# Up projections of a conv-gated FFN: high weights against high and low activations in one matmul of 512 columns

## The chip, the cores and the metric

The kernel runs on one core of one Trainium2 chip. The metric is the device time of one execution in microseconds (us). Before the change it is 771.88 us, the median of three runs (771.77 to 773.24).

## What is computed

The program is a decoder trunk of two layers over 256 tokens and a model width of 1024: a Mamba-2 mixer and an FFN, then shared keys and values, a dilated attention and a second FFN, and a last RMSNorm. The change is in the up projections of the two FFNs. All inputs and outputs are float32.

```
D_MODEL, SEQ, FFN_DIM, FFN_CONV = 1024, 256, 2816, 3

def _conv_ffn(h, w_up, conv_w, w_down):
    u = _causal_depthwise_conv(h @ w_up, conv_w)
    gate, val = u[..., :FFN_DIM], u[..., FFN_DIM:]
    return (jax.nn.silu(gate) * val) @ w_down

x = x + _conv_ffn(_rms_norm(x, ffn_norm[layer]), ffn_w_up[layer], ffn_conv_w[layer], ffn_w_down[layer])
```

## The kernel before

Every large product is done in three matmuls of a reduced-precision float32 type (F32R in the code). A weight tile is split into a high part `wh` (a cast on ScalarE, L98) and a low part `wl` (the weight minus its high part, on DVE, L100). The activations are split in the same way into `xnh` and `xnl`. The product is high times high, plus high weights times low activations, plus low weights times high activations; the low times low part is left out. L273, L274 and L275 (in `mm3`) are these three, each with 128 rows of contraction, 128 output channels and 256 columns, the tokens.

An up projection has 44 tiles of 128 channels. They are taken as 22 pairs, j = 0 to 21: tile j of the gate half and tile j of the value half. One DMA brings the weights of a pair (1 MB). A tile takes eight steps, k = 0 to 7, of three matmuls, so a pair takes 16 steps or 48 matmuls. Both tiles of a pair lie in the two halves of one PSUM bank of the tag `acc`, of which there are three. Pairs 0 to 4 multiply activations that are not yet normalised, and the result is scaled after (`u`, L729). In the place of pair 1 the function `normed` makes `xnh` and `xnl` from the normalised activations, and pairs 5 to 21 use these. That is 17 pairs in each layer.

After its matmuls a pair is worked off by `post` (L725): a first tap of the causal convolution on ScalarE for each tile (L311), two more taps for each tile on DVE (L317), a SiLU of the gate on ScalarE (L732), the product of both on DVE (`gf`, L734), and its split into high and low on ScalarE (L738) and DVE (L739), in the tile `gp`. For pairs 5 to 21 the convolution reads PSUM directly.

The weights run ahead of the matmuls. `W.get` for pair j also starts the DMA and the split of pair j + 1 in program order. There are three buffers for raw weights and six each for `wh` and `wl`, so three pairs. The order of instructions on TensorE is that of the code; on ScalarE and DVE a scheduler fixes it when the program is built, and each of these engines then works through its list strictly in that order. The DMAs of weights are issued on SyncE's queue.

The down projection that follows (`res_proj` in layer 0, `out_proj` in layer 1) reads `gp`, whose high and low parts lie next to each other. In `res_proj` (L665, L667) the high weights meet both parts in one matmul of 512 columns, and the low weights meet the high part in one of 256. In layer 1 `turn` transposes parts of the stream X on TensorE behind the matmuls of pairs 6 to 9, into PSUM banks of the tags t1, t2, t4 and t5.

Of the kernel before, what the change touches and what calls it, by code (L numbers as in the profile page):

```python
# [7 lines left out]
F32 = mybir.dt.float32  # L8
# [45 lines left out]
def trunk(ctx, tc, a, out):  # L54
# [145 lines left out]
    class Stream:  # L200
# [5 lines left out]
        def begin(self):  # L206
            self.h = []
            self.l = []
            for i in range(len(self.ws)):
                self.h.append(act.tile([128, KT, T], F32R, tag=f"xh{i}", name="xh"))  # L210
                self.l.append(act.tile([128, KT, T], F32R, tag=f"xl{i}", name="xl"))
            self.acc = act.tile([128, T], F32, tag="sqacc", name="sqacc")
# [94 lines left out]
    def conv(dst, u, w, b, taps):  # L307

        for i in range(2):
            if b is None:  # L310
                ACT.activation(out=dst[:, i, :], in_=u[:, i, :], func=AF.Copy, scale=w[i][:, taps - 1:taps])  # L311
            else:
                ACT.activation(out=dst[:, i, :], in_=u[:, i, :], func=AF.Identity,  # L313
                               scale=w[i][:, taps - 1:taps], bias=b[i])
        for i in range(2):
            for s in range(1, taps):
                r = DVE.scalar_tensor_tensor(out=dst[:, i, s:], in0=u[:, i, :T - s],  # L317
                                             scalar=w[i][:, taps - 1 - s:taps - s],
                                             in1=dst[:, i, s:], op0=ALU.mult, op1=ALU.add)
        return r  # L320

    def normed(w, rb):

        h = act.tile([128, KT, T], F32R, tag="xh1", name="xnh")
        l = act.tile([128, KT, T], F32R, tag="xl1", name="xnl")
        for k in range(KT):
            t = wk.tile([128, T], F32, tag="sq", name="xnt")
            DVE.scalar_tensor_tensor(out=t, in0=X[:, k, :], scalar=P(w)[:, k:k + 1], in1=rb,
                                     op0=ALU.mult, op1=ALU.mult)
            ACT.copy(out=h[:, k, :], in_=t)  # L330
            DVE.tensor_tensor(out=l[:, k, :], in0=t, in1=h[:, k, :].bitcast(F32), op=ALU.subtract)
        return h, l

# [3 lines left out]
    def operands():  # L337

        h = act.tile([128, KT, T], F32R, tag="xh1", name="xnh")
        l = act.tile([128, KT, T], F32R, tag="xl1", name="xnl")  # L340
        for i in range(2):
# [146 lines left out]
    def conv_post(g, n):  # L488
        st = sts[g]
        u = st["po" + n]  # L490
        cv = wk.tile([128, 2, T], F32, tag="cv" + n, name="cv")
# [221 lines left out]
    def ffn(L, S, nxt):  # L713
# [3 lines left out]
        po = {}  # L717
        cw = P(f"fconv{L}")

        def mm(j, i, **kw):  # L720
            if j not in po:
                po[j] = (acc_bank(), W.get(f"w_up{L}", j))
            tile_a(po[j][0][:, i, :], po[j][1][i], *ops[j >= 5], **kw)

        def post(j):  # L725
            u = po[j][0]
            if j < 5:
                u = wk.tile([128, 2, T], F32, tag="C", name="u")
                DVE.tensor_tensor(out=u, in0=po[j][0], in1=nm.row2, op=ALU.mult)  # L729
            cv = wk.tile([128, 2, T], F32, tag="cvbc", name="cv")  # L730
            conv(cv, u, [cw[:, 3 * t:3 * t + 3] for t in (j, j + FT)], None, 3)
# [10 lines left out]
        for j in range(FT):  # L742
# [11 lines left out]
            if j == 1:  # L754
                ops.append(normed(f"ffn_norm{L}", nm.row))
            if nxt is None and 5 < j < 10:
# [221 lines left out]
    def turn(i):  # L978

        c, f = i % 2, i // 2  # L980
        if i == 0:
            tok["x"] = act.tile([128, 2, D], F32, tag="xh0", name="xt")
            tok["w"] = act.tile([128, 2, D], F32, tag="xl0", name="wf")
            SP.dma_start(out=tok["w"][:, 0, :], in_=a["fnorm"].unsqueeze(0).to_broadcast([128, D]))
        pt = ps.tile([128, 512], F32, tag=f"t{(1, 2, 4, 5)[i]}", name="pxt")
        for n in range(4):
# [191 lines left out]
```

## Time and profile before

| what | value |
|---|---|
| median of three runs | 771.88 us |
| the profiled execution, its own time | 771.69 us |
| its span, first to last instruction | 769.6 us |
| TensorE busy | 758.8 us, 99% of the span |
| DVE busy | 605.4 us, 79% |
| ScalarE busy | 461.3 us, 60% |
| DMA bytes | 135.71 MB, mean 176 GB/s |

The profiled execution takes 2.1 us outside of its span and lies 0.2 us under the median. A matmul's listed duration reaches from its start to its modelled end, and the next one starts long before that end; so TensorE's pace is to be read from starts, and its busy share doesn't say how many matmuls it could take in the same time. Durations of DVE and ScalarE overlap a little too: the next instruction's start comes before the listed end of the one ahead.

### The profile page before, as it was taken

The numbers are of one execution on the slowest core, as the hardware profiler recorded it, in microseconds if no ns is written. First come the engines' busy times: TensorE is split into PE (matmuls) and PEld (weight loads), VectorE is DVE, ScalarE is ACT, GpSimd is POOL, SyncE is SP. The second block draws the span as 40 slices with busy tenths as digits, with TensorE's granted clock in tenths as the row PEclk, the third lists the DMA queues.
The fourth block names the chain that finished last, engine by engine and source line by source line (L and its number), as shares of the span: only waits on it lengthen the run. The fifth ranks groups of instructions, "written<-read, shape, count | busy, mean of one in ns | idle before, by whom it ended". The sixth has DMA issues, their size and how long they took to land.

```text
span 769.6 us, 14590 instructions
## 1 busy us (share of the span) xinstructions
PE 758.8 (99%) x5832; PEld 720.5 (94%) x5832; DVE 605.4 (79%) x1062; ACT 461.3 (60%) x776; POOL 97.7 (13%) x89
## 2 busy tenths in 40 slices
PE   8999999999999999999999999999999999999996
PEld 6899999999989999999888999999999999999885
DVE  6989988887588998887677598777588998888452
ACT  6757777775656566565556446556367676565331
POOL 0003635355100000000000131111100000000000
PEclk9999999999999999999999999999999999999999
DMA  8584753433272475545566654353234575554621
GB/s 324 200 301 158 288 187 111 165 110 121 99 278 106 169 270 183 201 151 172 184 206 230 204 175 157 108 192 121 100 118 158 195 271 172 192 185 143 220 75 55
DMA packets 22916, 135.71 MB, mean 176 GB/s; under 512 B 2561, under 2 KB 3873, under 8 KB 8769
## 3 DMA queue, kind: packets, MB, share of 16 engines
q1 hardware_dynamic: 21072, 129.51, 48.3%
q10 hardware_dynamic: 1776, 5.28, 2.0%
q8 instruction: 46, 0.75, 0.4%
q14 instruction: 22, 0.17, 0.1%
HBM read 133.17 MB, written 1.61 MB: 175 GB/s over the span
## 4 chain that ended last, share of the span: by engine, by line
PE 93%; issue 2%; DVE 2%; ACT 1%; DMA 1%; POOL 1%; SPq 0%; POOLq 0%; DVEq 0%
PE po L273 18%; PE po L275 18%; PE po L274 18%; PE po L665 7%; PE po L673 6%; PE po L667 4%; PE fo L1036 2%; PE fo L1037 2%; PE fo L1038 2%; PE py L568 1%; PE po L293 1%; PE po L294 1%; PE po L295 1%; PE s L903 1%; PE s L896 1%
## 5 line engine op out<-in xcount | busy, mean ns | idle before, releaser
L98 ACT CAST wh<-raw 128x1024 fp32r<-128x1024 f32 (+1 forms) x238 | 245.2, 1042 | 201.4 <-PE po L274 114.6
L100 DVE TENSOR_TENSOR wl<-raw,wh 128x1024 fp32r<-128x1024 f32 (+1 forms) x238 | 293.4, 1237 | 78.8 <-ACT wh L98 77.3
L273 PE MATMUL po<-xnh,wh 128*128 128x256 f32 x800 | 226.5, 283 | 0.0
L275 PE MATMUL po<-xnh,wl 128*128 128x256 f32 x800 | 226.0, 282 | 0.0
L274 PE MATMUL po<-xnl,wh 128*128 128x256 f32 x800 | 225.3, 282 | 0.0
L273 PEld LDWEIGHTS po<-xnh,wh 128*128 128x128 f32 x800 | 150.9, 189 | 0.2 <-issue 0.2
L274 PEld LDWEIGHTS po<-xnl,wh 128*128 128x128 f32 x800 | 151.0, 189 | 0.0
L275 PEld LDWEIGHTS po<-xnh,wl 128*128 128x128 f32 x800 | 150.1, 188 | 0.0
L273 PE MATMUL po<-xh,wh 128*128 128x256 f32 x400 | 115.3, 288 | 0.0
L275 PE MATMUL po<-xh,wl 128*128 128x256 f32 x400 | 113.1, 283 | 0.0
L274 PE MATMUL po<-xl,wh 128*128 128x256 f32 x400 | 112.8, 282 | 0.0
L317 DVE SCALAR_TENSOR_TENSOR cv<-po,prm,cv 128x255 f32<-128x255 f32 (+2 forms) x232 | 106.1, 476 | 5.1 <-ACT cv L313 2.8
L273 PEld LDWEIGHTS po<-xh,wh 128*128 128x128 f32 x400 | 76.1, 190 | 1.6 <-issue 1.5
L274 PEld LDWEIGHTS po<-xl,wh 128*128 128x128 f32 x400 | 76.2, 191 | 0.1
L275 PEld LDWEIGHTS po<-xh,wl 128*128 128x128 f32 x400 | 75.8, 190 | 0.0
L665 PE MATMUL po<-gp,wh 128*128 128x512 f32 x176 | 61.4, 392 | 0.0
L667 PE MATMUL po<-gp,wl 128*128 128x256 f32 x176 | 49.3, 280 | 0.0
L251 POOL TENSOR_TENSOR rcol<-ms,nhalf 128x2 f32<-128x2 f32 x5 | 6.4, 1282 | 274.5 <-DVE ms L248 274.5
L665 PEld LDWEIGHTS po<-gp,wh 128*128 128x128 f32 x176 | 33.0, 187 | 7.5
L1036 PE MATMUL fo<-wh,gp 128*128 128x512 f32 x88 | 34.5, 392 | 0.0
L1037 PE MATMUL fo<-wh,gp 128*128 128x512 f32 x88 | 34.5, 392 | 0.0
L1038 PE MATMUL fo<-wl,gp 128*128 128x512 f32 x88 | 34.5, 392 | 0.0
(226 smaller groups left out, 1246.6 us busy)
## 6 DMA issues: line engine op xcount, KB each, us to landing
raw<-w_up SPq DMA_DIRECT2D x44, 1024.0 KB, 4.9
raw<-w_down SPq DMA_DIRECT2D x18, 1024.0 KB, 4.9
raw<-w_xs SPq DMA_DIRECT2D x8, 1024.0 KB, 5.9
raw<-w_bc SPq DMA_DIRECT2D x8, 1024.0 KB, 4.9
raw<-w_out SPq DMA_DIRECT2D x8, 1024.0 KB, 5.0
raw<-w_q SPq DMA_DIRECT2D x8, 1024.0 KB, 5.2
raw<-w_z SPq DMA_DIRECT2D x6, 1024.0 KB, 5.6
dec<-rows ACTq DMA_DIRECT2D x8, 512.0 KB, 5.4
```

What stands on the lines that cost most here:

```text
L98: ACT.copy(out=wh[:, :n], in_=raw)
L100: DVE.tensor_tensor(out=wl[:, :n], in0=raw, in1=wh[:, :n].bitcast(F32), op=ALU.subtract)
L273: PE.matmul(po, lhsT=wh, rhs=xh, start=start, stop=False, **kw)
L274: PE.matmul(po, lhsT=wh, rhs=xl, start=False, stop=False, **kw)
L275: PE.matmul(po, lhsT=wl, rhs=xh, start=False, stop=stop, **kw)
L317: r = DVE.scalar_tensor_tensor(out=dst[:, i, s:], in0=u[:, i, :T - s], scalar=w[i][:, taps - 1 - s:taps - s], in1=dst[:, i, s:], op0=ALU.m ...
L665: PE.matmul(p.rearrange("p c t -> p (c t)"), lhsT=wh[:, c], rhs=y.rearrange("p c t -> p (c t)"), start=st, stop=False, skip_group_check=True)
L667: PE.matmul(p[:, 1, :], lhsT=wl[:, c], rhs=y[:, 0, :], start=False, stop=sp, skip_group_check=True)
L673: PE.matmul(p[:, o, :], lhsT=l[:, c], rhs=y[:, x, :], start=st and q == 0 and not o, stop=sp and q == 2, skip_group_check=True)
L1036: PE.matmul(po[c], lhsT=x[:, 0, t], rhs=wh[:, o], start=k == 0, stop=False)
L1037: PE.matmul(po[c], lhsT=x[:, 1, t], rhs=wh[:, o], start=False, stop=False)
L1038: PE.matmul(po[c], lhsT=x[:, 0, t], rhs=wl[:, o], start=False, stop=k == FT - 1)
```

## The change

For pairs 5 to 21 of both layers, `wide_mm` takes the place of `tile_a`. The normalised activations lie in one tile `xn` (tag xx1) with the high and the low part as two halves, 8 KB apart in a partition. A step is then two matmuls: `wh` against both halves (512 columns, L733), and `wl` against the high half (256 columns, L735), which is added to the second half of the bank. Each tile has a whole bank: the first tile of a pair takes the pair's `acc` bank, the second a bank of the tags t1 or t2, in turn. In `post`, ScalarE copies the second half of each bank to SBUF (`lo`, L762), DVE adds the first half to it (L763), and the convolution reads `lo` in place of PSUM. `turn` uses only the banks t4 and t5. Other places that had the tags xh1 and xl1 now share the tile xx1. The tests on j and i in `wide` give true for every tile of pairs 5 to 21.

```diff
@@ -207,8 +207,13 @@
             self.h = []
             self.l = []
             for i in range(len(self.ws)):
-                self.h.append(act.tile([128, KT, T], F32R, tag=f"xh{i}", name="xh"))
-                self.l.append(act.tile([128, KT, T], F32R, tag=f"xl{i}", name="xl"))
+                if i:
+                    hl = act.tile([128, 2, KT, T], F32R, tag="xx1", name="xh")
+                    h, l = hl[:, 0], hl[:, 1]
+                else:
+                    h, l = (act.tile([128, KT, T], F32R, tag=f"{n}0", name=n) for n in ("xh", "xl"))
+                self.h.append(h)
+                self.l.append(l)
             self.acc = act.tile([128, T], F32, tag="sqacc", name="sqacc")
 
         def add(self, k):
@@ -308,36 +313,36 @@
 
         for i in range(2):
             if b is None:
-                ACT.activation(out=dst[:, i, :], in_=u[:, i, :], func=AF.Copy, scale=w[i][:, taps - 1:taps])
+                ACT.activation(out=dst[:, i, :], in_=u[i], func=AF.Copy, scale=w[i][:, taps - 1:taps])
             else:
-                ACT.activation(out=dst[:, i, :], in_=u[:, i, :], func=AF.Identity,
+                ACT.activation(out=dst[:, i, :], in_=u[i], func=AF.Identity,
                                scale=w[i][:, taps - 1:taps], bias=b[i])
         for i in range(2):
             for s in range(1, taps):
-                r = DVE.scalar_tensor_tensor(out=dst[:, i, s:], in0=u[:, i, :T - s],
+                r = DVE.scalar_tensor_tensor(out=dst[:, i, s:], in0=u[i][:, :T - s],
                                              scalar=w[i][:, taps - 1 - s:taps - s],
                                              in1=dst[:, i, s:], op0=ALU.mult, op1=ALU.add)
         return r
 
     def normed(w, rb):
 
-        h = act.tile([128, KT, T], F32R, tag="xh1", name="xnh")
-        l = act.tile([128, KT, T], F32R, tag="xl1", name="xnl")
+        hl = act.tile([128, 2, KT, T], F32R, tag="xx1", name="xn")
+        h, l = hl[:, 0], hl[:, 1]
         for k in range(KT):
             t = wk.tile([128, T], F32, tag="sq", name="xnt")
             DVE.scalar_tensor_tensor(out=t, in0=X[:, k, :], scalar=P(w)[:, k:k + 1], in1=rb,
                                      op0=ALU.mult, op1=ALU.mult)
             ACT.copy(out=h[:, k, :], in_=t)
             DVE.tensor_tensor(out=l[:, k, :], in0=t, in1=h[:, k, :].bitcast(F32), op=ALU.subtract)
-        return h, l
+        return hl
 
 
     xh = act.tile([128, KT, T], F32R, tag="xh0", name="xh")
     xl = act.tile([128, KT, T], F32R, tag="xl0", name="xl")
     def operands():
 
-        h = act.tile([128, KT, T], F32R, tag="xh1", name="xnh")
-        l = act.tile([128, KT, T], F32R, tag="xl1", name="xnl")
+        hl = act.tile([128, 2, KT, T], F32R, tag="xx1", name="xn")
+        h, l = hl[:, 0], hl[:, 1]
         for i in range(2):
             t = act.tile([128, 4, T], F32, tag=f"dec{2 + i}", name="xnt")
             for k in range(0, 4, 2):
@@ -487,7 +492,7 @@
 
     def conv_post(g, n):
         st = sts[g]
-        u = st["po" + n]
+        u = [st["po" + n][:, i, :] for i in range(2)]
         cv = wk.tile([128, 2, T], F32, tag="cv" + n, name="cv")
         ti = (16 + g, 24 + g) if n == "bc" else (2 * g, 2 * g + 1)
         st["end"] = conv(cv, u, [P("convw")[:, 4 * t:4 * t + 4] for t in ti],
@@ -716,17 +721,47 @@
         g = []
         po = {}
         cw = P(f"fconv{L}")
+        xn = []
+
+        def wide_mm(j, i):
+
+            b = ps.tile([128, 2, T], F32, tag=("t1", "t2")[j % 2], name="pw") if i else po[j][0]
+            po[j][2][i] = b
+            wh, wl = po[j][1][i]
+            for k in range(KT):
+                c = slice(k * 128, k * 128 + 128)
+                PE.matmul(b.rearrange("p c t -> p (c t)"), lhsT=wh[:, c], rhs=xn[0][:, :, k, :],
+                          start=k == 0, stop=False, skip_group_check=True)
+                PE.matmul(b[:, 1, :], lhsT=wl[:, c], rhs=xn[0][:, 0, k, :], start=False, stop=k == KT - 1,
+                          skip_group_check=True)
+
+        def wide(j, i):
+            return j >= 5 and (i == 1 or True)
 
         def mm(j, i, **kw):
             if j not in po:
-                po[j] = (acc_bank(), W.get(f"w_up{L}", j))
-            tile_a(po[j][0][:, i, :], po[j][1][i], *ops[j >= 5], **kw)
+                po[j] = (acc_bank(), W.get(f"w_up{L}", j), {})
+            if wide(j, i):
+                return wide_mm(j, i)
+            if j < 5:
+                x = ops[0]
+            else:
+                x = xn[0][:, 0], xn[0][:, 1]
+            tile_a(po[j][0][:, i, :], po[j][1][i], *x, **kw)
 
         def post(j):
             u = po[j][0]
             if j < 5:
                 u = wk.tile([128, 2, T], F32, tag="C", name="u")
                 DVE.tensor_tensor(out=u, in0=po[j][0], in1=nm.row2, op=ALU.mult)
+            u = [u[:, i, :] for i in range(2)]
+            if j >= 5:
+                lw = wk.tile([128, 2, T], F32, tag="C", name="lo")
+            for i, b in po[j][2].items():
+                lo = lw[:, i, :]
+                ACT.copy(out=lo, in_=b[:, 1, :])
+                DVE.tensor_tensor(out=lo, in0=b[:, 0, :], in1=lo, op=ALU.add)
+                u[i] = lo
             cv = wk.tile([128, 2, T], F32, tag="cvbc", name="cv")
             conv(cv, u, [cw[:, 3 * t:3 * t + 3] for t in (j, j + FT)], None, 3)
             ACT.activation(out=cv[:, 0, :], in_=cv[:, 0, :], func=AF.Silu)
@@ -752,7 +787,7 @@
                 post(0)
             post(j)
             if j == 1:
-                ops.append(normed(f"ffn_norm{L}", nm.row))
+                xn.append(normed(f"ffn_norm{L}", nm.row))
             if nxt is None and 5 < j < 10:
                 turn(j - 6)
 
@@ -982,7 +1017,7 @@
             tok["x"] = act.tile([128, 2, D], F32, tag="xh0", name="xt")
             tok["w"] = act.tile([128, 2, D], F32, tag="xl0", name="wf")
             SP.dma_start(out=tok["w"][:, 0, :], in_=a["fnorm"].unsqueeze(0).to_broadcast([128, D]))
-        pt = ps.tile([128, 512], F32, tag=f"t{(1, 2, 4, 5)[i]}", name="pxt")
+        pt = ps.tile([128, 512], F32, tag=f"t{(4, 5, 4, 5)[i]}", name="pxt")
         for n in range(4):
             PE.transpose(pt[:, n * 128:n * 128 + 128], X[:, 4 * f + n, c * 128:c * 128 + 128], ident)
         ACT.copy(out=tok["x"][:, c, 512 * f:512 * f + 512], in_=pt)
```

The rows below are DVE's list in layer 0 before the change, from pair 4's `gf` on. `wl` rows are splits of weights, `cv<-po` the taps of pairs 5 and 6.

```order
L734 TENSOR_TENSOR gf<-cv 128x256
L317 SCALAR_TENSOR_TENSOR cv<-po,prm,cv 128x255
L100 TENSOR_TENSOR wl<-raw,wh 128x1024
L739 TENSOR_TENSOR gp<-gf,gp 128x256
L317 SCALAR_TENSOR_TENSOR cv<-po,prm,cv 128x254
L317 SCALAR_TENSOR_TENSOR cv<-po,prm,cv 128x255
L100 TENSOR_TENSOR wl<-raw,wh 128x1024
L317 SCALAR_TENSOR_TENSOR cv<-po,prm,cv 128x254
L100 TENSOR_TENSOR wl<-raw,wh 128x1024
L734 TENSOR_TENSOR gf<-cv 128x256
L317 SCALAR_TENSOR_TENSOR cv<-po,prm,cv 128x255
L100 TENSOR_TENSOR wl<-raw,wh 128x1024
```

This is the same stretch with the change. `lo<-po` is the addition for a pair's first tile and `lo<-pw` that for its second.

```order
L769 TENSOR_TENSOR gf<-cv 128x256
L763 TENSOR_TENSOR lo<-po,lo 128x256
L763 TENSOR_TENSOR lo<-pw,lo 128x256
L100 TENSOR_TENSOR wl<-raw,wh 128x1024
L774 TENSOR_TENSOR gp<-gf,gp 128x256
L322 SCALAR_TENSOR_TENSOR cv<-lo,prm,cv 128x255 x2
L322 SCALAR_TENSOR_TENSOR cv<-lo,prm,cv 128x254 x2
L100 TENSOR_TENSOR wl<-raw,wh 128x1024
L769 TENSOR_TENSOR gf<-cv 128x256
L763 TENSOR_TENSOR lo<-po,lo 128x256
L763 TENSOR_TENSOR lo<-pw,lo 128x256
L774 TENSOR_TENSOR gp<-gf,gp 128x256
```

Ahead of the taps of each pair stand two additions, and the taps of a pair stand together; one split of weights stands ahead of the taps and one behind them. Up to this place DVE's list is the same as before, and so it is in the parts of the program outside of pairs 5 to 21.

On ScalarE the list before, in the same place, reads as follows (`cv<-u` is the first tap of pair 4, `cv<-po` that of pair 5, `wh` are casts of weights):

```order
L311 ACTIVATE cv<-u,prm 128x256 x2
L98 CAST wh<-raw 128x1024
L732 ACTIVATE cv<-cv 128x256
L311 ACTIVATE cv<-po,prm 128x256 x2
L98 CAST wh<-raw 128x1024
L738 CAST gp<-gf 128x256
L98 CAST wh<-raw 128x1024
```

With the change it reads:

```order
L316 ACTIVATE cv<-u,prm 128x256 x2
L762 COPY lo<-po 128x256
L98 CAST wh<-raw 128x1024
L767 ACTIVATE cv<-cv 128x256
L762 COPY lo<-pw 128x256
L98 CAST wh<-raw 128x1024
L773 CAST gp<-gf 128x256
L316 ACTIVATE cv<-lo,prm 128x256 x2
```

The copy of a pair's second tile (`lo<-pw`), which can only run when the pair's last matmul is done, stands ahead of a cast of weights, of the cast to `gp` of the pair before, and of the first taps.

## Rows read from the trace of the kernel before

**Rows 1.** The page: busy time of the engines, and the granted clock in tenths.
```profile
PE 758.8 (99%) x5832; PEld 720.5 (94%) x5832; DVE 605.4 (79%) x1062; ACT 461.3 (60%) x776; POOL 97.7 (13%) x89
...
PEclk9999999999999999999999999999999999999999
```

**Rows 2.** Windows: pairs 5 to 21 of layer 0, then of layer 1.
```profile
core 0: us, PE busy (x) PEld busy (x) DVE busy (x) ACT busy (x) POOL busy (x), PEclk, DMA share, GB/s
256.97:354.89 97.92, 97.92 (x819) 97.92 (x818) 87.02 (x144) 60.30 (x104) 0.00 (x0) 1.00 0.58 202
602.64:702.30 99.66, 99.66 (x835) 99.66 (x834) 87.07 (x143) 62.62 (x108) 0.00 (x0) 1.00 0.60 207
```

**Rows 3.** Timeline of TensorE (start us, us) in layer 0's down projection.
```profile
359.79 0.39 PE L665 MATMUL po<-gp,wh 128*128 128x512 f32 x1
360.02 0.28 PE L667 MATMUL po<-gp,wl 128*128 128x256 f32 x1
360.14 0.39 PE L665 MATMUL po<-gp,wh 128*128 128x512 f32 x1
...
365.70 0.39 PE L665 MATMUL po<-gp,wh 128*128 128x512 f32 x1
```

**Rows 4.** Tile `xnh`: ns min/median/max, first and last start; layer 0, layer 1.
```profile
L273 PE MATMUL po<-xnh,wh x272: 278/280/283, 257.0 to 354.5; 128*128 128x256 f32 x136
L275 PE MATMUL po<-xnh,wl x272: 279/282/286, 257.2 to 354.8; 128*128 128x256 f32 x136
...
L273 PE MATMUL po<-xnh,wh x272: 278/282/369, 602.6 to 701.9; 128*128 128x256 f32 x136
```

**Rows 5.** Tile `gp` in layer 0's down projection, same columns.
```profile
L665 PE MATMUL po<-gp,wh x176: 389/391/422, 354.9 to 415.9; 128*128 128x512 f32 x176
L667 PE MATMUL po<-gp,wl x176: 278/280/297, 355.1 to 416.2; 128*128 128x256 f32 x176
```

**Rows 6.** Groups by line, whole program, shapes apart: busy us, mean ns.
```profile
L685 DVE TENSOR_TENSOR X<-po,X 128x256 f32<-128x256 f32 x36 | 14.4, 420 | 8.0 <-PE po L673 5.3 <-PE po L667 2.5
...
L522 PE MATMUL pg<-cv 128*128 128x256 f32 x16 | 4.9, 387 | 0.3 <-ACT cv L419 0.3
...
L941 PE MATMUL op<-pts,V 128*128 128x256 f32 x16 | 4.1, 379 | 0.0
...
L527 ACT COPY gs<-pg 128x256 f32<-128x256 f32 x8 | 2.9, 362 | 0.0
```

**Rows 7.** Timeline of DVE, layer 1, from pair 4's `u` on.
```profile
604.68 0.69 DVE L729 TENSOR_TENSOR u<-po,rbc 128x512 f32<-128x512 f32 x1
605.28 1.22 DVE L100 TENSOR_TENSOR wl<-raw,wh 128x1024 fp32r<-128x1024 f32 x1
606.41 0.42 DVE L739 TENSOR_TENSOR gp<-gf,gp 128x256 fp32r<-128x256 f32 x1
606.75 1.67 DVE L317 SCALAR_TENSOR_TENSOR cv<-u,prm,cv 128x255 f32<-128x255 f32 x4
608.33 1.22 DVE L100 TENSOR_TENSOR wl<-raw,wh 128x1024 fp32r<-128x1024 f32 x1
609.46 0.42 DVE L734 TENSOR_TENSOR gf<-cv 128x256 f32<-128x256 f32 x1
609.80 0.48 DVE L317 SCALAR_TENSOR_TENSOR cv<-po,prm,cv 128x255 f32<-128x255 f32 x1
...
612.23 0.43 DVE L739 TENSOR_TENSOR gp<-gf,gp 128x256 fp32r<-128x256 f32 x1 [0.82 <-ACT gp L738]
```

**Rows 8.** Timeline of ScalarE there.
```profile
610.84 1.05 ACT L98 CAST wh<-raw 128x1024 fp32r<-128x1024 f32 x1 [1.40 <-DMA raw<-w_up]
```

**Rows 9.** ScalarE's casts of weights, layer 0: busy, mean, idle before.
```profile
L98 ACT CAST wh<-raw 128x1024 fp32r<-128x1024 f32 x34 | 35.7, 1051 | 30.6 <-PE po L274 29.5 <-DMA raw<-w_up 1.1
```

## The prediction, made blind

> **What bounds the kernel now.** I read the busy shares first, then the windows of the changed stretch, then single starts on TensorE. TensorE is busy 99% of the span at a granted clock of nine tenths or more in every slice, so at its upper level, 2.4 GHz [rows 1], and in both stretches of pairs 5 to 21 it is busy without a break at a clock of 1.00, while DVE is busy 87 of 98 to 100 us and ScalarE 60 to 63 [rows 2]. TensorE sets the time there. But the 0.28 us of a matmul of 256 columns is not its price, since the next one starts 0.12 us later: L667 at 360.02, and the next at 360.14 [rows 3]. Whoever takes durations for prices finds 3 x 0.28 = 0.84 us for a step of three matmuls and 0.39 + 0.28 = 0.67 us for one of two, and a gain of 0.17 us for each of 544 steps, 92 us in all. The starts say otherwise.
>
> From starts: in layer 0 the 17 pairs are 3 x 272 = 816 matmuls, the first starting at 257.0 and the last at 354.8 [rows 4] (the 272 on the low activations are not shown). That is 97.8 us / 815 = 0.1200 us each, 0.360 us for a step and 5.76 us for a pair of 16 steps.
>
> **TensorE's part of the change.** It removes one matmul of 256 columns in every step and makes another one 512 columns wide. The down projection has this very pair of matmuls, in the same shapes and types, so I take the price there. Inside of it 17 steps run from 359.79 to 365.70, 0.3476 us each, of which the wide matmul holds 0.23 and the narrow one 0.12 [rows 3]. Over the whole stretch, with its changes of tile, 176 steps run from 354.9 to the last start at 416.2; less the last step's 0.23 this is 61.07 / 175 = 0.349 us [rows 5]. The saving is between 0.360 - 0.349 = 0.011 and 0.360 - 0.3476 = 0.0124 us. With 2 layers x 17 pairs x 2 tiles x 8 k = 544 steps it is 6.0 to 6.7 us. I take 6.4, or 0.0118 for a step. A pair then takes 16 x 0.348 = 5.57 us. Columns stay the same, 768 in a step; what goes is the fixed part of one matmul.
>
> The new moving operand is in two pieces 8 KB apart, which the down projection's is not. No row shows this for the reduced-precision type. In float32 a matmul of 256 columns in two pieces is listed at 379 ns (L941) and one in a single piece at 387 (L522) [rows 6]; these are durations, but nothing in them speaks for a price of the second piece. I take none. The upper bound is the whole saving.
>
> **What is added on ScalarE and DVE.** Each tile gets a copy out of PSUM on ScalarE, as L527, 0.36 us, and an addition on DVE, as L685, which also adds PSUM to SBUF at 128x256, 0.42 us listed [rows 6]. ScalarE has 60.30 / 17 = 3.55 us of work in a pair [rows 2]; with 0.72 more it is 4.3 of 5.57, so it stays off the path.
>
> DVE is the engine to look at. Where it waits for nothing, the starts give the prices: split of weights 605.28 to 606.41, 1.13; `gp` 0.34; four taps 606.75 to 608.33, 1.58; split 1.13; `gf` 0.34 [rows 7]. A pair is 4.52 us. Two additions at `gf`'s step of 0.34 make 5.20, at the full 0.42 5.36. Both stay below TensorE's 5.57, at 93 or 96%. So in the steady state I cost them at nothing; the cover is DVE's idle time of 0.2 to 0.4 us in a pair, and without it each 0.1 us in a pair would cost 34 x 0.1 = 3.4 us.
>
> That the weights are far ahead today shows in the casts, which sat idle 29.5 us in this stretch until a matmul released a buffer [rows 9]. So TensorE has a reserve before a late split reaches it, except at the start, where DVE comes out of `normed` and pairs 0 to 4 with a backlog. I walk there, in layer 1, where ScalarE also waits for raw weights. Pair 5 starts at 602.6 [rows 4] and with the change ends at 608.2, pair 6 at 613.8. DVE's list is the same as before up to `gf` of pair 4 at 609.46, so the second split for pair 6, started at 608.33, ends at 609.55 [rows 7]; TensorE needs it at 608.2 + 2.8 = 611.0. Then come two additions from 609.80 to 610.48, the first split for pair 7 to 611.6 (needed at 613.8), and `gp`, which before started at 612.23 because ScalarE's cast stood behind a cast of weights that waited for its DMA until 610.84 [rows 7, 8]; I leave it there. The taps end at 614.15, the second split for pair 7 at 615.4, needed at 613.8 + 2.8 = 616.6. That leaves 1.2 us, the least margin on the way, and each later pair adds some 0.3. Layer 0 has the same lists.
>
> **The added waits.** The copy of a pair's second tile waits on ScalarE for the pair's end; behind it stand a cast of weights two or three pairs ahead, the cast to `gp` and the first taps. DVE's second addition waits for that copy; behind it stand the split two pairs ahead and the taps. Both were so before in kind, as the first taps also waited for the pair's end. The bank of the second tile (t1 or t2) is free after the second addition, some 2 us after the pair's end, and wanted 5.57 + 2.8 = 8.4 us after it; the `acc` bank is now free earlier than before, when all taps had to be done with it. `turn` reuses t4 and t5 two pairs after a copy of under 1 us: nothing. The DMA rate wanted is 1.05 MB in 5.57 us, 188 GB/s, and these stretches ran at 202 and 207 [rows 2]. Nothing outside of the two stretches changes its order.
>
> **The sum.** The profiled execution, 771.7 us (its span of 769.6 and 2.1 around it), less 6.4 is 765.3. The median of the runs is 0.2 above it: 771.9 - 6.4 = 765.5, a gain of 0.8%.
>
> **The rivals.**
>
> *A backlog at the start reaches TensorE.* For it: the margin of 1.2 us hangs on DMAs and on ScalarE's list. If the additions and the waits in front of them put DVE 2 to 4 us later than I walked, TensorE stands 1 to 3 us in each layer: 767.5 to 771.5. Against it: the walk already holds the wait for the DMA.
>
> *The step doesn't get shorter.* If the second piece of the operand starts anew and pays the fixed part again, a step stays at 0.360 us and the time at 771.9. For it: no row has this operand. Against it: the durations of L941 and L522 [rows 6]. The Trainium skill, in "TensorE: Matmul & The Clock Gate", section "Back-to-back issue gap", would leave nearly nothing to gain too: it gives columns / 2.4 + 2.5 ns between isolated matmuls, so by it the change saves 2.5 ns a step, an estimate of 1.4 us and 770.5. This case's rows disagree: 0.120 us between starts where the rule gives 0.109, and 0.23 where it gives 0.216 [rows 3, 4]; the fixed part here is about 13 ns, and I go by the rows.
>
> *DVE becomes the bound, and the kernel is slower.* DVE's busy time today is 87.02 / 17 = 5.12 us in a pair [rows 2], more than the 4.52 of its unbroken starts, since taps wait for the taps ahead of them and for ScalarE. If none of this gives way and the additions cost 0.42 each, a pair takes 5.96 us and TensorE follows: 34 x (5.96 - 5.76) = 6.8 us more, 778.7. It decides against the change from 5.76 us in a pair on. For it: DVE is the fullest engine after TensorE. Against it: its pauses are there because it has nothing to do, and in the new list the taps stand by twos, so that none follows at once on the one it needs.
>
> **How the numbers follow.** Forecast 0.76, backlog 0.08, no shorter step 0.07 (of which 0.03 for a gain of 1.4 us at most), DVE bound 0.09. The forecast's own range is 765.2 to 765.9 by the bounds of the step. The range of 764.3 to 769.0 takes half a microsecond and more on either side for other executions, and half of the backlog case. About 0.2%, 1.5 us, is what a measurement of this kernel can tell from no change. Faster by more than this: the forecast and most of the backlog case, 0.83. Within it: 0.08. Slower: 0.09.
>
> **What would show it.** In the profile after, L733 and L735 should start 0.23 and 0.12 us apart, and pairs 5 to 21 should take 94.7 us in layer 0 against 97.9. DVE's busy time should grow by 23 to 28 us to about 630, with no wait of TensorE for DVE or ScalarE in the stretch. A backlog would show as gaps in TensorE's starts at pairs 6 to 9. A price of the second piece would show as over 0.24 us behind L733. I am wrong if DVE's pair stays above 5.57 us to the end of a stretch.

## The result, and the profile after

| | before | after |
|---|---|---|
| median | 771.86 us (4 runs, 771.77 to 773.24) | 766.28 us (4 runs, 765.74 to 766.44) |
| ratio | | 0.992, 95% interval 0.9908 to 0.9933 |
| span of the profiled execution | 769.6 us | 764.5 us |
| TensorE busy, matmuls | 758.8 us, 5832 | 753.4 us, 5288 |
| DVE busy | 605.4 us | 622.8 us |
| ScalarE busy | 461.3 us | 484.3 us |

The change gains 5.6 us, 0.7%. The forecast was 765.5 us, a gain of 6.4.

The page of the changed kernel, busy times and granted clock, answers to [rows 1]:

```profile
PE 753.4 (99%) x5288; PEld 690.9 (90%) x5288; DVE 622.8 (81%) x1130; ACT 484.3 (63%) x844; POOL 97.6 (13%) x89
...
PEclk9999999999999999999999999999999999999998
```

544 matmuls are gone and the clock is the same. Where the time went shows in the windows of pairs 5 to 21, layer 0 and layer 1, with the columns of [rows 2]:

```profile
257.23:352.46 95.23, 95.23 (x546) 83.14 (x545) 94.12 (x176) 72.02 (x138) 0.00 (x0) 1.00 0.59 204
...
600.20:697.23 97.03, 97.03 (x563) 84.78 (x562) 95.53 (x175) 73.50 (x141) 0.00 (x0) 1.00 0.61 211
```

The stretches take 95.23 us for 97.92 and 97.03 for 99.66: 2.69 and 2.63, together 5.3 us, which is all of the 5.1 by which the span is shorter. The medians lie 5.6 apart since an execution took 2.1 us beyond its span before (771.69 for 769.6) and takes 1.8 now (766.27 for 764.5); these 0.3 us aren't a matter of the steps, and their cause was not followed. TensorE still works without a break. DVE, the third busy time, now fills 94.12 of 95.23 us. That looks like a bound, and the experiments say whether it is one.

TensorE's starts in pair 6 of layer 0 (start us, us):

```profile
262.86 0.39 PE L733 MATMUL po<-xn,wh 128*128 128x512 f32 x1
263.09 0.28 PE L735 MATMUL po<-xn,wl 128*128 128x256 f32 x1
263.21 0.39 PE L733 MATMUL po<-xn,wh 128*128 128x512 f32 x1
...
265.66 0.39 PE L733 MATMUL pw<-xn,wh 128*128 128x512 f32 x1
...
268.46 0.39 PE L733 MATMUL po<-xn,wh 128*128 128x512 f32 x1
```

The wide matmul holds TensorE for 0.23 us and the narrow one for 0.12, as forecast. But a tile of eight steps takes 2.80 us (262.86 to 265.66, and again to 268.46), so a step takes 0.350 and not the 0.348 that the forecast put into a pair. Before it was 0.360 [rows 4].

DVE's list in the same pair, and the place of layer 1 where the walk saw the least margin (start us, us):

```profile
264.10 0.41 DVE L769 TENSOR_TENSOR gf<-cv 128x256 f32<-128x256 f32 x1
264.43 0.41 DVE L763 TENSOR_TENSOR lo<-po,lo 128x256 f32<-128x256 f32 x1
264.77 0.41 DVE L763 TENSOR_TENSOR lo<-pw,lo 128x256 f32<-128x256 f32 x1
265.10 1.21 DVE L100 TENSOR_TENSOR wl<-raw,wh 128x1024 fp32r<-128x1024 f32 x1
266.23 0.41 DVE L774 TENSOR_TENSOR gp<-gf,gp 128x256 fp32r<-128x256 f32 x1
266.57 1.66 DVE L322 SCALAR_TENSOR_TENSOR cv<-lo,prm,cv 128x255 f32<-128x255 f32 x4
268.14 1.22 DVE L100 TENSOR_TENSOR wl<-raw,wh 128x1024 fp32r<-128x1024 f32 x1
269.28 0.42 DVE L769 TENSOR_TENSOR gf<-cv 128x256 f32<-128x256 f32 x1
...
600.79 1.21 DVE L100 TENSOR_TENSOR wl<-raw,wh 128x1024 fp32r<-128x1024 f32 x1
...
611.09 1.21 DVE L100 TENSOR_TENSOR wl<-raw,wh 128x1024 fp32r<-128x1024 f32 x1
```

From one `gf` to the next are 5.18 us, and the additions start 0.33 and 0.34 us apart. In the view of the tile `xn` (ns min/median/max, first and last start) the stretch of layer 0 reaches from 257.2 to 352.3, 95.1 us from its first start to its last; several runs are measured against it:

```profile
L733 PE MATMUL po<-xn,wh x136: 389/394/422, 257.2 to 349.3; 128*128 128x512 f32 x136
...
L735 PE MATMUL pw<-xn,wl x136: 279/279/279, 260.3 to 352.3; 128*128 128x256 f32 x136
```

ScalarE's groups in layer 0's stretch (busy us, mean ns, idle us before them and releasers) answer to [rows 9]:

```profile
L98 ACT CAST wh<-raw 128x1024 fp32r<-128x1024 f32 (+1 forms) x35 | 36.5, 1044 | 10.3 <-PE po L733 3.9 <-PE pw L733 3.2 <-DMA raw<-w_up 3.0
...
L762 ACT COPY lo<-po 128x256 f32<-128x256 f32 x17 | 6.1, 362 | 2.0 <-PE po L735 2.0
L762 ACT COPY lo<-pw 128x256 f32<-128x256 f32 x16 | 5.9, 369 | 1.8 <-PE pw L735 1.8
```

The casts of weights sat idle for 30.6 us in this stretch before and for 10.3 now: the weights still run ahead of TensorE, but by less.

### The profile page after: what moved, and what is told of

The parts are those of the page before. It is cut to its first block, busy times and chain, and to the rows that moved or that the text cites. A ratio compares the mean times of both kernels' runs of the same rounds, so it can differ in the third digit from the quotient of the medians.

```text
span 764.5 us, 13565 instructions
## 1 busy us (share of the span) xinstructions
PE 753.4 (99%) x5288; PEld 690.9 (90%) x5288; DVE 622.8 (81%) x1130; ACT 484.3 (63%) x844; POOL 97.6 (13%) x89
## 4 chain that ended last, share of the span: by engine, by line
PE 93%; issue 2%; DVE 2%; ACT 1%; DMA 1%; POOL 1%; SPq 0%; POOLq 0%; DVEq 0%
PE po L278 10%; PE po L279 10%; PE po L280 10%; PE po L733 8%; PE pw L733 8%; PE po L670 7%; PE po L678 6%; PE po L735 4%; PE pw L735 4%; PE po L672 4%; PE fo L1071 2%; PE fo L1073 2%; PE fo L1072 2%; PE py L573 1%; PE po L298 1%
## 5 line engine op out<-in xcount | busy, mean ns | idle before, releaser
L278 PE MATMUL po<-xh,wh 128*128 128x256 f32 x400 | 115.3, 288 | 0.0
L733 PE MATMUL po<-xn,wh 128*128 128x512 f32 x272 | 97.1, 394 | 0.0
L733 PE MATMUL pw<-xn,wh 128*128 128x512 f32 x272 | 96.7, 393 | 0.0
L735 PE MATMUL po<-xn,wl 128*128 128x256 f32 x272 | 75.9, 279 | 0.0
L735 PE MATMUL pw<-xn,wl 128*128 128x256 f32 x272 | 75.9, 279 | 0.0
L278 PE MATMUL po<-xn,wh 128*128 128x256 f32 x256 | 73.1, 286 | 0.0
L280 PE MATMUL po<-xn,wl 128*128 128x256 f32 x256 | 72.2, 282 | 0.0
L279 PE MATMUL po<-xn,wh 128*128 128x256 f32 x256 | 72.0, 281 | 0.0
L322 DVE SCALAR_TENSOR_TENSOR cv<-lo,prm,cv 128x255 f32<-128x255 f32 (+1 forms) x136 | 61.7, 476 | 0.3
L733 PEld LDWEIGHTS pw<-xn,wh 128*128 128x128 f32 x272 | 51.0, 187 | 12.2
L733 PEld LDWEIGHTS po<-xn,wh 128*128 128x128 f32 x272 | 51.0, 187 | 11.9
L279 PE MATMUL po<-xl,wh 128*128 128x256 f32 x208 | 58.8, 283 | 0.0
L279 PE MATMUL po<-xh,wh 128*128 128x256 f32 x192 | 54.0, 281 | 0.0
L735 PEld LDWEIGHTS po<-xn,wl 128*128 128x128 f32 x272 | 51.0, 188 | 0.0
L735 PEld LDWEIGHTS pw<-xn,wl 128*128 128x128 f32 x272 | 51.0, 187 | 0.0
```

Source lines behind the costliest of these rows:

```text
L278: PE.matmul(po, lhsT=wh, rhs=xh, start=start, stop=False, **kw)
L279: PE.matmul(po, lhsT=wh, rhs=xl, start=False, stop=False, **kw)
L280: PE.matmul(po, lhsT=wl, rhs=xh, start=False, stop=stop, **kw)
L322: r = DVE.scalar_tensor_tensor(out=dst[:, i, s:], in0=u[i][:, :T - s], scalar=w[i][:, taps - 1 - s:taps - s], in1=dst[:, i, s:], op0=ALU.m ...
L733: PE.matmul(b.rearrange("p c t -> p (c t)"), lhsT=wh[:, c], rhs=xn[0][:, :, k, :], start=k == 0, stop=False, skip_group_check=True)
L735: PE.matmul(b[:, 1, :], lhsT=wl[:, c], rhs=xn[0][:, 0, k, :], start=False, stop=k == KT - 1, skip_group_check=True)
```

## The experiments

The kernel before was run beside each; its median was 771.8 to 772.0 us throughout. All edits are against the changed kernel, a ratio is to the kernel before, and `...` in an edit stands for lines that are not shown.

**1. The operand in one piece.** High and low activations of one k lie next to each other, as in the down projection.

```diff
-        hl = act.tile([128, 2, KT, T], F32R, tag="xx1", name="xn")
-        h, l = hl[:, 0], hl[:, 1]
+        hl = act.tile([128, KT, 2, T], F32R, tag="xx1", name="xn")
+        h, l = hl[:, :, 0, :], hl[:, :, 1, :]
...
-                PE.matmul(b.rearrange("p c t -> p (c t)"), lhsT=wh[:, c], rhs=xn[0][:, :, k, :],
+                PE.matmul(b.rearrange("p c t -> p (c t)"), lhsT=wh[:, c], rhs=xn[0][:, k].rearrange("p c t -> p (c t)"),
...
```

> The high and low activations of a k lie next to each other (128 x 8 x 2 x 256), so that the wide matmul reads one piece of 512 columns; nothing else differs from the changed kernel. Theory 1, the second piece 8 KB away costs about 3 ns in each wide matmul: the wide matmul holds TensorE 0.230 us and not 0.233, 544 x 0.003 = 1.6 us less, 764.7 us. Theory 2, the 3 ns come from the banks or from waits: no change, 766.3 us.

Measured: 766.36 us (765.88 to 766.41), ratio 0.9926 [0.9913, 0.994]. In the view of the tile `xn` the stretch of layer 0 reaches from 256.8 to 352.0, as long as in the changed kernel within 0.1 us:

```profile
L733 PE MATMUL po<-xn,wh x136: 389/393/422, 256.8 to 348.9; 128*128 128x512 f32 x136
...
L735 PE MATMUL pw<-xn,wl x136: 278/279/280, 259.9 to 352.0; 128*128 128x256 f32 x136
```

So the second piece costs nothing, which the prediction had assumed, and the missing 2 ns of a step lie elsewhere. The first theory falls.

**2. Only the second tile of each pair.**

```diff
-            return j >= 5 and (i == 1 or True)
+            return j >= 5 and i == 1
```

> Only the second tile of a pair is wide, the first goes as before. Theory 1, the gain is a fixed part for each step: half of the 544 steps, half of the 5.6 us, 769.1 us. Theory 2, the gain comes with something else in the changed pairs, such as PSUM banks that are free earlier: not half, either 766.3 or near 771.9 us.

Measured: 769.03 us (768.74 to 770.39), ratio 0.9964 [0.9952, 0.9977]. The gain goes with the number of steps: 272 of them give 2.8 us, 544 give 5.6. The first theory holds.

**3. All of the change but the wide matmul.** Banks, copies, additions and order stay; `wh` meets the two parts in two matmuls of 256 columns.

```diff
-                PE.matmul(b.rearrange("p c t -> p (c t)"), lhsT=wh[:, c], rhs=xn[0][:, :, k, :],
-                          start=k == 0, stop=False, skip_group_check=True)
+                PE.matmul(b[:, 0, :], lhsT=wh[:, c], rhs=xn[0][:, 0, k, :], start=k == 0, stop=False,
+                          skip_group_check=True)
+                PE.matmul(b[:, 1, :], lhsT=wh[:, c], rhs=xn[0][:, 1, k, :], start=False, stop=False,
+                          skip_group_check=True)
```

> Everything as in the changed kernel (tile, banks, copies, additions), but the wide matmul is issued as two of 256 columns with the same weights, into the two halves of the bank. Theory 1, the gain is the fixed part of the matmul that was merged: a step is back at 0.360 us and the time at 771.5 to 772. Theory 2, banks or waits made the gain: it stays near 766.3 us.

Measured: 771.66 us (771.46 to 772.79), ratio 0.9999 [0.999, 1.0008]. The view of `xn` in layer 0:

```profile
L733 PE MATMUL po<-xn,wh x136: 277/280/283, 257.1 to 351.8; 128*128 128x256 f32 x136
...
L737 PE MATMUL pw<-xn,wl x136: 279/283/287, 260.2 to 354.9; 128*128 128x256 f32 x136
```

(354.9 - 257.1) / 815 is 0.1200 us from start to start, the price of before, so what shortens the two stretches is the merging alone; 68 copies and 68 additions more cost nothing. The matmul that was merged took its own load of weights with it (5832 loads before and 5288 after, the same as the matmuls), so its "fixed part" here is that of both: no run takes the one away without the other. And this kernel too takes 1.8 us beyond its span (771.5 for 769.7), so the 0.3 us outside of the span come with something else of the change.

**4. Without copies and additions.** The convolution reads the first half of each bank, so the two low terms of these products are left out.

```diff
-                lo = lw[:, i, :]
-                ACT.copy(out=lo, in_=b[:, 1, :])
-                DVE.tensor_tensor(out=lo, in0=b[:, 0, :], in1=lo, op=ALU.add)
-                u[i] = lo
+                u[i] = b[:, 0, :]
```

> The convolution reads the first half of each bank directly; copies and additions are left out, and with them the two low terms of the up projections of pairs 5 to 21. Theory 1, copies and additions are hidden beside TensorE: 766.3 us as with them, within 0.5. Theory 2, they hold TensorE up a little and are what the gain fell short by: 1 us less, 765.2 us.

Measured: 766.38 us (766.18 to 767.73), ratio 0.9934 [0.9921, 0.9946]. The stretch of layer 0 in the view of `xn`, and a window around it:

```profile
L733 PE MATMUL po<-xn,wh x136: 389/393/423, 257.1 to 349.2; 128*128 128x512 f32 x136
...
L735 PE MATMUL pw<-xn,wl x136: 279/279/280, 260.2 to 352.3; 128*128 128x256 f32 x136
...
257.10:352.60 95.50, 95.50 (x547) 83.23 (x546) 88.34 (x147) 61.33 (x107) 0.00 (x0) 1.00 0.61 208
```

DVE is busy 6 us less in this stretch (88.34 for 94.12) and ScalarE 11, and the time is the same, 257.1 to 352.3 for 257.2 to 352.3. The added work is hidden whole.

**5 and 6. How much room DVE has.** Additions of 128x256 that nobody reads, one more in a pair (5) and two (6); the edit for two is shown, and for one `range(1 - i)` stands in the place of `range(1)`.

```diff
                 u[i] = lo
+                for _ in range(1):
+                    xt = wk.tile([128, T], F32, tag="sq", name="xtra")
+                    DVE.tensor_tensor(out=xt, in0=lo, in1=lo, op=ALU.add)
```

> One more addition of 128x256 on DVE in every pair, into scratch that nobody reads (the output is unaffected). With two, TensorE stood still once in three pairs and three pairs took 17.8 us, so DVE's pair was 5.93 us, and 5.25 without them. Theory 1, so much is DVE's whole work: with one more 5.59 us against TensorE's 5.60, which is just hidden: 766.3 to 767. Rival, DVE's pair stretches to whatever TensorE leaves and the bound came from elsewhere (the order of the list): half of the loss, about 771.

> Two more additions of 128x256 on DVE in every pair, behind those of the change, into scratch that nobody reads (the output is unaffected). It asks how much room DVE has left. Theory 1, DVE's unbroken list of a pair is 5.18 us against 5.60 on TensorE: with 2 x 0.34 more it is 5.86 us, DVE becomes the bound, and each of the 34 pairs takes up to 0.26 us more, 8.8 us less what the weights split ahead give (about 2 us in each layer): 770 to 775. Rival, DVE's 94 of 95 us are stretched by waiting and it has more room than its list says: unchanged, 766.3.

Measured: with one more 767.0 us (766.83 to 769.39), ratio 0.9938 [0.9924, 0.9953]; with two 777.68 us (776.08 to 778.37), ratio 1.007 [1.0057, 1.0083]. TensorE's starts with two more (start us, us, idle before), in the first tile of a pair of layer 0:

```profile
287.33 0.39 PE L733 MATMUL po<-xn,wh 128*128 128x512 f32 x1
288.39 0.38 PE L735 MATMUL po<-xn,wl 128*128 128x256 f32 x1 [0.67 <-DVE wl L100]
```

The narrow matmul comes 1.06 us behind the wide one and not 0.23: it waited for the low weights. The same wait stands at 306.21, 324.16 and 341.97, three pairs apart. From 288.39 to 341.97 are nine pairs, 5.95 us each. So DVE's pair takes 5.95 - 0.68 = 5.27 us in the changed kernel, where TensorE takes 5.60, and 5.61 with one more, which is at the edge. The room is 0.33 us in a pair, one addition. With one more the first theory holds, and the loss of 0.7 us can be found. Layer 0's stretch takes 95.6 us for 95.1: the first tiles of pairs 7, 11 and 21 are 0.11 to 0.16 us longer there, each with its first narrow matmul 0.06 us behind the end of the split that it reads. Layer 1's takes 96.9 as without it, and the down projection of layer 0 takes 0.3 us more. With two the loss came out larger than expected, 11.4 us; in the two stretches it is 7.5 us (99.6 and 99.9 from the first to the last start, for 95.1 and 96.9), and the down projections behind them wait for low weights too, 1.0 and 0.6 us. What is left lies outside of these places and was not followed.

Run 5, with one more, shows something else, in the down projection behind the stretch. No tile of a matmul lies elsewhere in it than in the changed kernel, and the matmuls and their order are the same. TensorE's starts at steps 17 and 43 of the first two tiles there, and at the same steps of the next two:

```profile
359.00 0.39 PE L670 MATMUL po<-gp,wh 128*128 128x512 f32 x1
...
368.18 0.40 PE L670 MATMUL po<-gp,wh 128*128 128x512 f32 x1
...
374.50 0.39 PE L670 MATMUL po<-gp,wh 128*128 128x512 f32 x1
...
383.52 0.39 PE L670 MATMUL po<-gp,wh 128*128 128x512 f32 x1
```

26 steps take 9.18 us, 0.353 each, and then 9.02, 0.3467 each. In the changed kernel it is 0.3467 in both places (12). The slower run of steps stands behind a step that was held up (358.48 to 359.00, 0.52 us). So one and the same list of matmuls, on the same addresses, has more than one pace; this matters for run 12.

**7, 8 and 9. Other orders of the same matmuls.** The first step of each tile in three matmuls; odd steps with the narrow matmul ahead; a tile's eight wide ones first and then its eight narrow ones. Of the first two edits the added lines are shown.

```diff
+                for q in range(2) if k == 0 else ():
+                    PE.matmul(b[:, q, :], lhsT=wh[:, c], rhs=xn[0][:, q, k, :], start=q == 0, stop=False,
+                              skip_group_check=True)
+                if k:
+                    PE.matmul(b.rearrange("p c t -> p (c t)"), lhsT=wh[:, c], rhs=xn[0][:, :, k, :],
+                              start=False, stop=False, skip_group_check=True)
```

```diff
+                for q in (0, 1) if k % 2 == 0 else (1, 0):
+                    last = k == KT - 1 and q == 0
+                    if q == 0:
+                        PE.matmul(b.rearrange("p c t -> p (c t)"), lhsT=wh[:, c], rhs=xn[0][:, :, k, :],
+                                  start=k == 0, stop=last, skip_group_check=True)
+                    else:
+                        PE.matmul(b[:, 1, :], lhsT=wl[:, c], rhs=xn[0][:, 0, k, :], start=False, stop=last,
+                                  skip_group_check=True)
```

```diff
                 PE.matmul(b.rearrange("p c t -> p (c t)"), lhsT=wh[:, c], rhs=xn[0][:, :, k, :],
                           start=k == 0, stop=False, skip_group_check=True)
+            for k in range(KT):
+                c = slice(k * 128, k * 128 + 128)
                 PE.matmul(b[:, 1, :], lhsT=wl[:, c], rhs=xn[0][:, 0, k, :], start=False, stop=k == KT - 1,
                           skip_group_check=True)
```

> The first step of every tile in three matmuls of 256 columns, the other seven as changed. In the changed kernel a tile's eight steps take 2800 ns again and again (350.0 a step), in the down projection long runs of the same pair of matmuls take 346.7 a step and others 350.0. Theory 1, the 350.0 is a rhythm in which TensorE stays until something breaks it, and 3 matmuls break it: 3 x 120 + 7 x 346.7 = 2787 ns for a tile, 68 tiles save 0.9 us, about 765.4. Rival, 350.0 is simply what the pair of matmuls costs in this stretch: 2810 ns for a tile, 0.7 us more, about 767.0.

> In every odd step the narrow matmul stands ahead of the wide one, so that matmuls of one width stand by twos; same matmuls, same columns. Theory 1, the 3.3 ns a step over 346.7 hang on the alternation of widths or on the rhythm: half of them or all go, 544 x 1.7 to 3.3 ns, 764.5 to 765.4. Rival, they are the price of this stretch (its DMAs, its operands): unchanged, 766.3.

> A tile's eight wide matmuls first, then its eight narrow ones; same matmuls, same columns. Theory 1, alternation costs: wide behind wide starts 227 ns apart in the last projection of the program, narrow behind narrow 120, so 8 x 347 = 2776 ns for a tile against 2800 and 68 x 0.024 = 1.6 us less, 764.7. Rival, the stretch costs it: unchanged, 766.3.

Measured: 766.93 us (766.57 to 768.33), 768.09 (767.47 to 768.33) and 768.26 (768.13 to 769.39). Starts of the third kernel, equal matmuls taken together (start us, us, count):

```profile
264.79 1.12 PE L737 MATMUL po<-xn,wl 128*128 128x256 f32 x8
265.75 2.03 PE L733 MATMUL pw<-xn,wh 128*128 128x512 f32 x8
267.62 1.12 PE L737 MATMUL pw<-xn,wl 128*128 128x256 f32 x8
```

Eight narrow ones hold TensorE for 0.96 us, 0.120 each as before, but eight wide ones in a row for 1.87, 0.234 each: 2.83 us for a tile, where taking turns gives 2.80. The mirrored order takes 2.83 too (its starts are not shown), and 68 x 0.027 = 1.8 us is what both lose. With three matmuls ahead a tile takes 2.81 and the kernel 766.93, as that run's rival said. In the other two both sides fall, since theory 1 said shorter and the rival unchanged: the pace depends on the order, but turns are the best order of those tried, and breaking them doesn't bring the 346.7 ns.

**10 and 11. Coming back to a bank.** The two tiles of a pair in turns of four steps (the edit shown), and in turn step by step (1 in place of 4).

```diff
+            for k, i in [(k, i) for s in range(0, KT, 4) for i in range(2) for k in range(s, s + 4)]:
+                b = bs[i]
+                wh, wl = po[j][1][i]
```

> The two tiles of a pair in turns of four steps: tile 0 k 0 to 3, tile 1 k 0 to 3, tile 0 k 4 to 7, tile 1 k 4 to 7; same matmuls, same columns. In the down projection a step takes 350.0 ns in the first eight k of a tile, which open the banks, and 346.7 from the point where TensorE comes back to a bank that is already begun, until the next tile begins. Theory 1, it is the return to a begun bank that brings the shorter rhythm: half of the 544 steps save 3.3 ns, 0.9 us, 765.4. Rival, it is something else (the wait for a new unit of weights, the operand): unchanged, 766.3.

> The two tiles of a pair in turn, step by step, so that 14 of a pair's 16 steps return to a begun bank; same matmuls, same columns. Theory 1, the return to a begun bank brings the shorter rhythm: 34 x 14 x 3.3 ns = 1.6 us less, 764.7. Rival, it is something else: unchanged, 766.3, or longer, if a change of bank in every step costs something. In both, the second tile's low weights are wanted some 2.5 us earlier than in the changed kernel, and DVE could come late for them at pairs 6 to 8; that would show as waits of TensorE there, and not as a longer step.

Measured: 766.74 us (766.48 to 768.63) and 769.22 (768.73 to 770.28). After the first pair eight steps take 2.80 us in both (but for pairs 6 to 9 of layer 1, where `turn` stands between), so it isn't the return to a bank. What the second kernel loses is a wait in pair 5 (start us, us, idle before):

```profile
257.71 0.39 PE L736 MATMUL pw<-xn,wh 128*128 128x512 f32 x1
259.24 0.38 PE L738 MATMUL pw<-xn,wl 128*128 128x256 f32 x1 [1.14 <-DVE wl L100]
```

1.53 us for 0.23, with another such wait at pair 5 of layer 1 (1.49 us): 2.6 us of the 2.9 that it loses. The low weights of pair 5 in the changed kernel, the split of each tile and the first matmul that reads it (start us, us):

```profile
255.13 1.21 DVE L100 TENSOR_TENSOR wl<-raw,wh 128x1024 fp32r<-128x1024 f32 x1
...
257.46 0.28 PE L735 MATMUL po<-xn,wl 128*128 128x256 f32 x1
...
257.84 1.21 DVE L100 TENSOR_TENSOR wl<-raw,wh 128x1024 fp32r<-128x1024 f32 x1
...
260.29 0.28 PE L735 MATMUL pw<-xn,wl 128*128 128x256 f32 x1
```

The splits end at 256.34 and 259.05, 1.1 and 1.2 us before they are wanted. These are the least margins of the stretch, at pair 5 and not at pair 7.

**12. The operand 32 bytes further.**

```diff
+        act.tile([128, 8], F32, tag="pad", name="pad")
         hl = act.tile([128, 2, KT, T], F32R, tag="xx1", name="xn")
```

> Eight floats are left free ahead of the tile of the normed activations, so that it and all that is placed behind it (the first four tiles of the down projection's operand among them) lie 32 bytes later in a partition; same instructions otherwise. In the down projection the operand's tiles for k 0 to 7 lie at multiples of 64 bytes and their steps take 350.0 ns, those for k 8 to 21 lie 32 bytes off such a multiple, as the weights do, and their steps take 346.7. The normed activations lie at a multiple of 64 bytes in the changed kernel. Theory 1, it is this place that costs 3.3 ns: the steps of the up projections and of the down projection's first eight k go to 346.7, 544 + some 100 steps save 2.1 us, 764.2. Rival, it is not the place modulo 64 (but the region of the memory, or the first eight k of a tile): 350.0 as before, 766.3.

Measured: 767.2 us (766.0 to 767.33), ratio 0.9934 [0.992, 0.9948]. Layer 0's stretch reaches from a first start at 257.1 to a last one at 352.5, 95.4 us, for 257.2 to 352.3 in the changed kernel: not shorter. What this expectation rests on is the down projection of the changed kernel. Its starts at step 0, at steps 16 and 17 (k is 8 from step 16 on), and at step 44, where the next two tiles begin:

```profile
352.46 0.39 PE L670 MATMUL po<-gp,wh 128*128 128x512 f32 x1
...
358.06 0.40 PE L670 MATMUL po<-gp,wh 128*128 128x512 f32 x1
...
358.42 0.39 PE L670 MATMUL po<-gp,wh 128*128 128x512 f32 x1
...
367.78 0.40 PE L670 MATMUL po<-gp,wh 128*128 128x512 f32 x1
```

The first 16 steps take 5.60 us, 0.350 each; the 27 from 358.42 take 9.36, 0.3467 each. With the shift steps 17 and 44 read so (start us, us):

```profile
358.57 0.40 PE L671 MATMUL po<-gp,wh 128*128 128x512 f32 x1
...
368.11 0.39 PE L671 MATMUL po<-gp,wh 128*128 128x512 f32 x1
```

27 steps in 9.54 us: 0.353 each, though this part of the operand (k from 8 on) lies where it lay. So the steps that were moved didn't go to 346.7, and steps that were not moved left it. The theory falls in this form. Nor does it follow that the shift itself set the new pace: run 5 has the same 0.353 in this place with nothing moved.

## Why the prediction came out right, and by how much it was off

**What bounds the kernel** was read rightly: TensorE, by starts and not by durations. The reckoning from durations that the prediction warned of, 92 us, is 16 times the gain.

**TensorE's part** is the mechanism: with the wide matmul split again the gain is gone (3), with half of the tiles half of it is there (2). That the gain is a matmul's fixed part and not that of the weight load that goes with it is argued, not shown. Its size was off. The forecast took 0.0118 us for a step, from rows of the down projection between 359.79 and 365.70 [rows 3] and from the mean of its stretch [rows 5]; measured are 0.360 - 0.350 = 0.0100 us, 5.4 us for 544 steps in place of 6.4. Of the 17 steps chosen 15 lie at k of 8 and more, where a step takes 0.3467; the first 16 steps of that same projection take 0.350, as those of the up projections do. The range of the step should have had 0.350 as its lower bound for the saving, and it was there to be read. The forecast's own range, 765.2 to 765.9, misses 766.28 by 0.4 us; the wider one holds it. A part of the nearness is luck: the sum kept 2.1 us outside of the span, they came out at 1.8, and without that the miss would be 0.7.

**Nothing for the second piece** was right (1). **Copies and additions at nothing** was right (4), and the reason given holds: DVE's unbroken pair is 5.18 us by the starts, forecast 5.20, and 5.27 by where it begins to bind (5 and 6); the margin is 0.33 us in a pair, forecast 0.2 to 0.4. DVE's busy time grew by 17.4 us and not by 23 to 28. The listed durations added up grew by 27.5 us (664.6 to 692.1 over the program), but they overlap by 10.1 us more (69.3 for 59.1).

**The rivals.** No backlog reached TensorE, but the least margin was at pair 5 and 1.1 us (11), ahead of the place where the walk began to look. At pair 7 of layer 1 it was wider than the 1.2 us walked: the second split, which starts at 611.09, ends at 612.30, and the matmul that reads it comes 2.6 us later (start us, us):

```profile
614.93 0.28 PE L735 MATMUL pw<-xn,wl 128*128 128x256 f32 x1
```

The walk had left out that `turn` stands behind pair 6, for which tiles there take up to 3.16 us. The DVE rival had its place right, and nearly its price: at 5.95 us in a pair TensorE waits and the kernel takes 777.68 us, for the 778.7 of the rival's 5.96 (6). It did not come true since the 5.12 us of busy time were stretched by pauses that gave way. The Trainium skill's rule for isolated matmuls in "TensorE: Matmul & The Clock Gate", section "Back-to-back issue gap", would have left a gain of 1.4 us, an estimate; 5.4 us were measured between runs that differ in the wide matmul alone (3), 10 ns for each matmul taken out.

**What stays open** is why a step takes 0.350 in the one place and 0.3467 in the other. It isn't the two pieces (1), the added work (4), the opening of a bank (10, 11), or the operand's place modulo 64 bytes alone (12). The same steps on the same addresses ran at 0.3467 and at 0.353 (5), so places alone don't set it; what happened just before, or what the other engines do meanwhile, is a rival that no run separates. Reaching 0.3467 in all 544 steps would be worth 1.8 us. None of the other orders and places of the same work is faster than the changed kernel.

## What to carry to other kernels

Price a matmul by the distance from its start to the next start, and look at that distance over a whole tile at several places before taking one as the price: here the same pair of matmuls takes 346.7, 350.0 or 353 ns, and the choice of rows cost 1.0 us of a gain of 6.4. Merging two matmuls that share their weights gives back one fixed part, here 10 ns, with the two operands side by side or 8 KB apart. What pays for it in additions is free only while the engine that adds keeps its pair below TensorE's; find that point by adding dummy work, since a busy share of 99% did not mean a bound here, and one addition more met it.

## What the runs showed of the hardware

- Two neighbouring matmuls don't have two independent prices. In turn the wide one holds 0.231 to 0.234 us and the narrow one 0.118, together 0.350; eight of each in a row take 0.234 and 0.120 each, together 0.353 (9). Three narrow ones take 0.120 each (3).
- The rhythm is exact over whole tiles: 2.80 us for eight steps, pair after pair, under DMAs of 204 and 211 GB/s and with DVE busy 94 of 95 us or 88 (4). Only the first tile of a stretch (2.84) and pairs 6 to 9 of layer 1, with `turn` between, take longer.
- The pace is not a property of the matmuls and their addresses alone. Steps of the down projection that take 0.3467 us in the changed kernel take 0.353 where other tiles were moved by 32 bytes (12), and 0.353 in one run of steps with nothing moved, behind a step that was held up (5). What sets it stays open.
